# A two-layer adaLN trunk on one core: modulation weights read transposed and summed along the free axis, and the first products visited row block by row block

## The chip, the cores and the metric

One core of one Trainium2 chip runs the whole program. The metric is the device time of one execution in microseconds (us), as the median of the runs shown. Matrix products run on TensorE (PE in the rows, PEld its weight loads), elementwise work on VectorE (DVE) and ScalarE (ACT), a little on GpSimd (POOL). SyncE (SP) issues most loads.

## The reference, cut to what matters

```python
def reference(x, c, norm_w, mod_w, mod_b, a_w_in, a_w_out, b_w_in, b_w_out, final_norm_w):
    cond = jax.nn.silu(c)                              # c: (1, 2048)
    for i in range(2):                                 # x: (1, 256, 2048)
        mod = cond @ mod_w[i] + mod_b[i]               # mod_w[i]: (2048, 3 * 2048)
        shift, scale, gate = jnp.split(mod[:, None, :], 3, axis=-1)
        h = rms_norm(x, norm_w[i]) * (1.0 + scale) + shift
        # layer 0: ten projections of 2048 columns; layer 1: four
        y = (dilated_mixer(h, a_w_in[0], slopes) @ a_w_out[0] if i == 0
             else moba_mixer(h, b_w_in[0], slopes) @ b_w_out[0])
        x = x + gate * y
    return rms_norm(x, final_norm_w)
```

All data are float32. Each layer reads its weights once, and modulation weights of 2 x 2048 x 6144 numbers (100 MB of the 377 MB read) serve one product with a single vector each.

## The kernel before

**Data on the chip.** h is held transposed: hA has 16 row blocks of 128 (the model dimension, index k or kc) by 256 tokens, each as a high and a low part of float32r. A weight unit is two row blocks by 512 columns, 512 KB. `convert` loads it into `raw` (a pool of five buffers, `rawp`, that modulation blocks share), ScalarE copies it to `wh` (L376) and VectorE subtracts to get `wl` (L383, "split" below). Four pairs of wh and wl exist (`NB`). A product of a unit is three products on TensorE per tile (high by high, low by high, high by low).

**Steps.** The program is a list of steps, each some products of one unit, written out by hand in one loop at the end: the products, then tasks due at once (`at_once`: copying sums out), the splits, loads of new units by a plan, and tasks set for that step (`at`). The engines' queues keep this order. Layer A works in four column groups j of ten parts (v0 to v2, z, q0 to k2). The **first stage** takes the 16 first parts (`first_parts`: all of group 0, six of group 1) over only some row blocks at a time, since h's modulation is not known at the start: five strips of 2, 4, 4, 4 and 2 row blocks (`STRIPS`, in units 1, 2, 2, 2, 1). After each strip a part's sums go from PSUM to `act` (`evac_partial`: ScalarE copies for the first strip, VectorE adds, L591, for the other four). The rest of layer A, the output projection, layer B and its output follow.

**Modulation before.** `mod_w` lies with its 2048 inputs over partitions. For a block, VectorE multiplies each row of inputs by its value of silu(c) (`ccT`, one per partition) and adds to an accumulator `macc` (`mac`, L134 and L136). At the end the 128 partitions are added up: TensorE transposes, VectorE reduces (`column_sums`, L194 and L195). The very first strip is loaded by eight `start_unit`s of 256 columns, with some of the sums on TensorE (L157, L162); later strips by `strip_unit` while the strip before is worked on, and `strip_end` then makes hA's row blocks (L296 to L298). The gate of layer 0 and shift and scale of layer 1 come in six `piece_unit` sequences spread over the rest of layer A, from 16 steps after the first stage; the gate of layer 1 in two, in layer B's groups 1 and 2. The gate is summed over partitions and spread over them by products with ones (`gate_end`, `gate_add`).

**Attention.** Eight items per group (`item_a`), each in four tasks: scores (L472), softmax, transposes (L453), values (L490). The first group's items begin five steps before the end of the first stage.

Of the kernel before, what the change touches and what calls it, by code (L numbers as in the profile page):

```python
# [17 lines left out]
P = 128  # L18
S = 256
# [33 lines left out]
def trunk_kernel(ctx: ExitStack, tc: tile.TileContext, x, c, norm_w, mod_w, mod_b, a_w_in, a_w_out,  # L53
                 b_w_in, b_w_out, final_norm_w, dmask, out):
# [10 lines left out]
    maccp = pool("maccp", 2)  # L65
# [17 lines left out]
    rows = tp.tile([P, 512], F32, name="t")  # L83
    rows_c, rows_n, rows_b, cs = rows[:KC, 0:P], rows[:2 * KC, P:2 * P], rows[:96, 2 * P:3 * P], rows[:KC, 3 * P:]
    nc.scalar.dma_start(rows_c, c.rearrange("o (k p) -> (o k) p", p=P))
    nc.scalar.dma_start(rows_n, norm_w.rearrange("l (k p) -> (l k) p", p=P))
    nc.scalar.dma_start(rows_b, mod_b.rearrange("l (k p) -> (l k) p", p=P))
    gate = const.tile([P, D], F32, name="gate")
    dm = const.tile([P, 9 * P], F32, name="dm")
    ident = const.tile([P, P], F32, name="ident")  # L90
    make_identity(nc, ident)
    ones = const.tile([P, P], F32, name="ones")
    nc.gpsimd.memset(ones, 1.0)
# [4 lines left out]
    ccT = const.tile([P, KC], F32, name="ccT")  # L98
    nwT = const.tile([P, 2 * KC], F32, name="nwT")
    mbT = const.tile([P, 96], F32, name="mbT")  # L100
    abB = const.tile([P, 2 * KC], F32, name="abB")
    ssp = const.tile([P, 8], F32, name="ssp")

    nc.scalar.activation(cs, rows_c, AF.Silu)
    pst = ps_t.tile([P, 512], F32, name="pst", tag="t")
    nc.tensor.transpose(pst[:, 0:KC], cs, ident[:KC, :KC])
    nc.vector.tensor_copy(ccT, pst[:, 0:KC])

    def start_rows():
        psn = ps_y.tile([P, 512], F32, name="psy", tag="y")  # L110
        nc.tensor.transpose(psn[:, 16:48], rows_n, ident[:32, :32])
        nc.tensor.transpose(psn[:, 48:144], rows_b, ident[:96, :96])
        nc.vector.tensor_copy(nwT, psn[:, 16:48])
        nc.vector.tensor_copy(mbT, psn[:, 48:144])
        for l in range(2):
            m1 = mbT[:, 48 * l + 16:48 * l + 32]
            nc.vector.tensor_scalar(m1, m1, 1.0, None, op0=ALU.add)
# [14 lines left out]
    def mac(acc, raw, kc, first):  # L132
        if first:
            nc.vector.tensor_scalar(acc, raw, ccT[:, kc:kc + 1], None, op0=ALU.mult)  # L134
        else:
            nc.vector.scalar_tensor_tensor(acc, raw, ccT[:, kc:kc + 1], acc, op0=ALU.mult, op1=ALU.add)  # L136

    STRIPS = [1, 2, 2, 2, 1]
    strip_acc = {}

    start_ps = ps_t.tile([P, 512], F32, name="pst", tag="t")

    start_acc = maccp.tile([P, 1024], F32, name="macc", tag="macc")

    def start_unit(u):

        part, i = 1 - u // 4, u % 4
        raw = rawp.tile([P, 4, 256], F32, name="raw", tag="raw")
        src = mod_w[0, i * 512:(i + 1) * 512, part * D:part * D + 256]
        nc.sync.dma_start(raw, src.rearrange("(c p) n -> p c n", p=P))  # L150
        for k in range(4):
            kc = 4 * i + k
            if u < 4 or 4 <= kc < 14:
                mac(start_acc[:, part * 256:(part + 1) * 256], raw[:, k], kc, (u, k) in ((0, 0), (5, 0)))
                continue
            for b in range(2):
                nc.tensor.matmul(start_ps[:, b:b + 1], raw[:, k, b * P:(b + 1) * P], ccT[:, kc:kc + 1],  # L157
                                 start=u == 4 and k == 0 and b == 0, stop=False, skip_group_check=True)
# [710 lines left out]
```

## Time and profile before

| | |
|---|---|
| median of 3 runs | 1601.39 us (1598.77 to 1601.77) |
| the profiled execution | 1597.84 us, its span 1596.0 us |
| TensorE busy | 1561.0 us, 98% of the span |
| VectorE busy | 1173.8 us, 74% |
| ScalarE busy | 756.8 us, 47% |
| moved by DMA | 380.75 MB, 239 GB/s over the span |
| issues | 192 blocks of mod_w, 512 units of the four weights, 512 KB each |

The span goes from the first to the last instruction; the execution's own time is 1.8 us more. A TensorE instruction's duration includes a pipelined end that lies under the next one, so its pace is read from the starts of neighbours or from counts per window, not from durations.

### The profile page before, as it was taken

Reading aid. Unit: us, or ns where it says so; the run is one execution under the profiler, and the core shown is the slowest. Engines: PE = TensorE matmul, PEld = TensorE weight load, DVE = VectorE, ACT = ScalarE, POOL = GpSimd, SP = SyncE. Lnnn points to the kernel's source line nnn. Section 1 sums busy time; section 2 is a strip of 40 time slices with the busy share of each in tenths; the row PEclk is TensorE's granted clock in tenths of the full one; section 3 lists DMA queues with packets and bytes.
Section 4 is the critical chain, followed back from the end, with each engine's and each line's share of the span. In section 5 each row is a group of like instructions: output and inputs, shape, how many; then the busy total and the mean of one; then the engine's idle time right before and its main releaser. Section 6 shows DMA issues by size and latency. Waiting matters only on the chain.

```text
span 1596.0 us, 23586 instructions
## 1 busy us (share of the span) xinstructions
PE 1561.0 (98%) x9055; PEld 1376.4 (86%) x9055; DVE 1173.8 (74%) x1597; ACT 756.8 (47%) x1039; POOL 12.0 (1%) x29
## 2 busy tenths in 40 slices
PE   5999999999999999999999999999999999999997
PEld 4899999999888888888888888887888888888886
DVE  6899898878767776777776776766557877765665
ACT  4643334334544544444544444554445555455543
POOL 0000000000000000000000000000000000000000
PEclk9999999999999999999999999999999999999999
DMA  9988798866378768888778888456466877855553
GB/s 309 320 273 293 248 313 272 254 214 186 114 230 296 221 206 285 289 307 296 223 234 266 310 292 282 132 195 200 159 194 228 281 249 248 279 181 186 185 168 122
DMA packets 182240, 380.75 MB, mean 239 GB/s; under 512 B 11616, under 2 KB 19952, under 8 KB 181616
## 3 DMA queue, kind: packets, MB, share of 16 engines
q1 hardware_dynamic: 180352, 373.93, 71.6%
q0 software_dynamic: 1008, 4.19, 0.8%
q8 instruction: 71, 1.16, 0.3%
q10 hardware_dynamic: 768, 1.12, 0.2%
q14 instruction: 41, 0.34, 0.1%
HBM read 377.10 MB, written 2.10 MB: 238 GB/s over the span
## 4 chain that ended last, share of the span: by engine, by line
PE 92%; DMA 3%; DVE 3%; ACT 1%; issue 1%; POOL 0%; POOLq 0%; DVEq 0%; ACTq 0%
PE acc L335 27%; PE acc L338 14%; PE acc L313 10%; PE acc L311 10%; PE acc L312 10%; PE acc L326 4%; PE acc L325 4%; PE acc L324 4%; DMA raw<-in_mod_w_dram 2%; PE pss L472 2%; PE po L490 1%; PE pst L453 1%; DVE macc L136 1%; PE po L523 1%; PE pss L507 1%
## 5 line engine op out<-in xcount | busy, mean ns | idle before, releaser
L376 ACT ACTIVATE wh<-raw 128x1024 fp32r<-128x1024 f32 x504 | 528.1, 1058 | 536.7 <-PE acc L335 125.8
L383 DVE TENSOR_TENSOR wl<-raw,wh 128x1024 fp32r<-128x1024 f32 (+1 forms) x505 | 607.1, 1218 | 115.8 <-ACT wh L376 114.8
L335 PE MATMUL acc<-hA,wh 128*128 128x512 f32 x1152 | 302.9, 395 | 0.0
L136 DVE SCALAR_TENSOR_TENSOR macc<-raw,ccT,macc 128x1024 f32<-128x1024 f32 (+2 forms) x264 | 247.2, 936 | 48.5 <-DMA raw<-in_mod_w_dram 44.8
L335 PEld LDWEIGHTS acc<-hA,wh 128*128 128x128 f32 x1152 | 202.3, 189 | 32.0
L335 PE MATMUL acc<-hB,wh 128*128 128x512 f32 x768 | 203.4, 396 | 0.0
L324 PE MATMUL acc<-hA,wh 128*128 128x256 f32 x640 | 182.2, 285 | 0.6 <-ACT ext L589 0.4
L338 PEld LDWEIGHTS acc<-hA,wl 128*128 128x128 f32 x1152 | 166.8, 189 | 18.0
L326 PE MATMUL acc<-hA,wl 128*128 128x256 f32 x640 | 181.1, 283 | 0.0
L325 PE MATMUL acc<-hA,wh 128*128 128x256 f32 x640 | 181.1, 283 | 0.0
L338 PE MATMUL acc<-hA,wl 128*128 128x256 f32 x1152 | 171.8, 281 | 0.0
L311 PE MATMUL acc<-wh,hA 128*128 128x512 f32 x384 | 155.5, 405 | 4.2 <-ACT hA L296 1.5
L335 PEld LDWEIGHTS acc<-hB,wh 128*128 128x128 f32 x768 | 135.5, 189 | 21.8
L312 PE MATMUL acc<-wl,hA 128*128 128x512 f32 x384 | 151.1, 393 | 0.3 <-DVE wl L383 0.3
L313 PE MATMUL acc<-wh,hA 128*128 128x512 f32 x384 | 150.9, 393 | 0.0
L324 PEld LDWEIGHTS acc<-hA,wh 128*128 128x128 f32 x640 | 122.8, 192 | 1.6 <-ACT ext L589 0.7
L325 PEld LDWEIGHTS acc<-hA,wh 128*128 128x128 f32 x640 | 122.8, 192 | 0.4
L326 PEld LDWEIGHTS acc<-hA,wl 128*128 128x128 f32 x640 | 122.7, 192 | 0.0
L338 PEld LDWEIGHTS acc<-hB,wl 128*128 128x128 f32 x768 | 111.1, 189 | 12.1
L338 PE MATMUL acc<-hB,wl 128*128 128x256 f32 x768 | 114.5, 281 | 0.0
L311 PEld LDWEIGHTS acc<-wh,hA 128*128 128x128 f32 x384 | 73.0, 190 | 19.0 <-ACT actA1v L589 1.6
L313 PEld LDWEIGHTS acc<-wh,hA 128*128 128x128 f32 x384 | 72.8, 189 | 15.8
(235 smaller groups left out, 1680.8 us busy)
## 6 DMA issues: line engine op xcount, KB each, us to landing
raw<-in_a_w_in_dram SPq DMA_DIRECT2D x320, 512.0 KB, 4.8
raw<-in_mod_w_dram SPq DMA_DIRECT2D x192, 512.0 KB, 4.9
raw<-in_b_w_in_dram SPq DMA_DIRECT2D x128, 512.0 KB, 4.3
raw<-in_a_w_out_dram SPq DMA_DIRECT2D x32, 512.0 KB, 4.6
raw<-in_b_w_out_dram SPq DMA_DIRECT2D x32, 512.0 KB, 4.3
xin<-in_x_dram SPq DMA_DIRECT2D x2, 1024.0 KB, 9.2
x<-in_x_dram POOLq DMA_DIRECT2D x4, 512.0 KB, 5.8
gate<-in_mod_b_dram SPq DMA_DIRECT2D x1, 1024.0 KB, 7.8
```

The costliest lines, as they stand in the source:

```text
L136: nc.vector.scalar_tensor_tensor(acc, raw, ccT[:, kc:kc + 1], acc, op0=ALU.mult, op1=ALU.add)
L311: nc.tensor.matmul(o, hi, wh[:, i], start=f, stop=False, skip_group_check=True)
L312: nc.tensor.matmul(o, hi, wl[:, i], start=False, stop=False, skip_group_check=True)
L313: nc.tensor.matmul(o, lo, wh[:, i], start=False, stop=l, skip_group_check=True)
L324: nc.tensor.matmul(o, wh[:, i, wc], hi, start=f, stop=False, skip_group_check=True)
L325: nc.tensor.matmul(o, wh[:, i, wc], lo, start=False, stop=False, skip_group_check=True)
L326: nc.tensor.matmul(o, wl[:, i, wc], hi, start=False, stop=l, skip_group_check=True)
L335: nc.tensor.matmul(ps_of(h), ws[u][0][:, i, cols(h)], both, start=us[u] == 0 and i == 0, stop=False, skip_group_check=True)
L338: nc.tensor.matmul(ps_of(h)[:, 0:S], ws[u][1][:, i, cols(h)], st(2 * us[u] + i)[:, 0, :], start=False, stop=us[u] == 7 and i == 1, skip_gr ...
L376: nc.scalar.activation(wh, raw, AF.Copy)
L383: nc.vector.tensor_tensor(wl[:, c], raw[:, c], wh[:, c].bitcast(F32), op=ALU.subtract)
L472: nc.tensor.matmul(ps[:, n:n + w], heads_of("A", j, f"q{g}")[:, hh, tok], heads_of("A", j, f"k{g}")[:, hh, ks], start=True, stop=True)
```

## The change

1. **Modulation along the free axis.** The host transposes mod_w: `mod_t` has, per layer and block of 128 outputs, the outputs over partitions and the 2048 inputs along a row, in two halves of 4 KB per partition. `cb` holds silu(c) on all partitions, made by four products of a row of ones with c and four Silu. `mod_unit` loads a half and issues two `tensor_tensor_reduce` (multiply by cb, sum over 512), each of which becomes an ISA instruction of 128x512 and a second one of 128x1 that writes the sum into `modq`; a bias enters as the first sum's start. `mod_sums` adds four quarters. No transposes of sums, no `macc`. The gate's column is turned into rows by products of ones with diagonal matrices (`gate_split`, `gate_rows`).
2. **Visits.** The first 16 parts are worked half-unit by half-unit (one row block by 512 columns). The table `READY` says at which half-step row block k is ready (0, 9, 18, 28, 39, 50, 62, then every 12 up to 170). A visit takes the part that is furthest behind as far as rows are ready. This gives 55 visits of 1 to 10 row blocks, where the strips had 80; 16 are first ones (copied by ScalarE), 39 add (23 of them by half-step 170). Row block k has its four modulation blocks between READY[k - 1] and READY[k], then `rows_ready(k)`: a sum, a product with the norm's weight, two ScalarE operations for hA's high part and the full value, one subtraction.
3. **Order and layout.** `weights` holds all units in the order of use, a unit as 4 KB per partition; before, a unit was two pieces of 2 KB per partition. x is loaded first, then four modulation blocks, then weights. Six scalings of x move from VectorE to POOL. The attention items of the first group begin at half-step 217 of 256, and the later pieces at half-step 170, spread to 12 steps before layer A's output. The gate of layer 1 comes in 64 steps on end.

The number of products of h with weights is the same, and so is the number of bytes of weights.

```diff
-    def strip_unit(s, u):
...
-        nc.sync.dma_start(raw, mod_w[0, i * n * P:(i + 1) * n * P, n0:n0 + w].rearrange("(c p) n -> p c n", p=P))
-        for k in range(n):
-            mac(strip_acc[s][:, part * w:(part + 1) * w], raw[:, k], i * n + k, i == 0 and k == 0)
+    for i, (p, t) in enumerate(zip((ps_y, ps_t, ps_s, ps_o), "ytso")):
+        pcb = p.tile([P, 512], F32, name="pcb", tag=t)
+        nc.tensor.matmul(pcb, ones[0:1], c_row[i // 2][0:1, i % 2 * 512:(i % 2 + 1) * 512], start=True, stop=True)
+        nc.scalar.activation(cb[:, i * 512:(i + 1) * 512], pcb, AF.Silu)
+    def mod_unit(layer, b, half):
+        raw = rawp.tile([P, 1024], F32, name="raw", tag="raw")
+        nc.sync.dma_start(raw, mod_t[layer, b, half])
+        m = 48 * layer + b
+        for i in range(2):
+            part, q = raw[:, i * 512:(i + 1) * 512], 2 * half + i
+            nc.vector.tensor_tensor_reduce(part, part, cb[:, q * 512:(q + 1) * 512], 1.0, 0.0 if q else mbT[:, m:m + 1],
+                                           ALU.mult, ALU.add, modq[:, m, q:q + 1])
+    def mod_sums(m, n, step=1):
+        cols = slice(m, m + (n - 1) * step + 1, step)
+        nc.vector.tensor_reduce(modc[:, cols], modq[:, cols], axis=AX.X, op=ALU.add)
...
         if g:
-            nc.vector.tensor_scalar(xc, xc, start_r[tt][:, 0:1], None, op0=ALU.mult)
+            nc.gpsimd.tensor_scalar(xc, xc, start_r[tt][:, 0:1], None, op0=ALU.mult)
...
+    def rows_ready(k):
+        mod_sums(k, 2, 16)
+        sc, sh = sc0[:, k:k + 1], modc[:, k:k + 1]
+        nc.vector.tensor_tensor(sc, modc[:, 16 + k:17 + k], nwT[:, k:k + 1], op=ALU.mult)
+        src = xnT[k // 8][:, k % 8]
+        hf = tmpp.tile([P, S], F32, name="hf", tag="tmp")
+        nc.scalar.activation(hA[:, k, 0], src, AF.Identity, scale=sc, bias=sh)
+        nc.scalar.activation(hf, src, AF.Identity, scale=sc, bias=sh)
+        nc.vector.tensor_tensor(hA[:, k, 1], hf, hA[:, k, 0].bitcast(F32), op=ALU.subtract)
...
-        nc.sync.dma_start(raw, units[n]["src"])
+        nc.sync.dma_start(raw, weights[n].rearrange("p (c n) -> p c n", c=2))
...
+    for n in (9, 9, 10, 11, 11) + (12,) * 10:
+        READY.append(READY[-1] + n)
...
+        n = done.index(min(done)) if n_ready < KC else next(i for i, d in enumerate(done) if d < KC)
+        k0 = done[n]
+        while done[n] < KC and READY[done[n]] <= t:
+            done[n] += 1
+            t += 1
+        visits.append((n, k0, done[n]))
...
+    for k in range(1, KC):
+        i0, i1 = READY[k - 1], READY[k]
+        for n in range(4):
+            at(i0 + n * (i1 - i0 - 3) // 4, mod_unit, 0, (16 if n < 2 else 0) + k, n % 2)
+        at(i1 - 3, rows_ready, k)
...
-            base = i0 - 5 + i if j == 1 else i0 + 1 + 2 * i
+            base = first_group_end + 2 + 3 * i if j == 1 else i0 + 1 + 2 * i
...
-    span = (first_end + 16, len(steps) - 8)
+    span = (READY[-1], len(steps) - 12)
```

Three places in the engines' queues, in program order. The first is SP's queue at its start, where the names are destination and source; before:

```order
L150 DMA raw<-in_mod_w_dram 128x4x256 x2
L253 DMA xin_107<-in_x_dram 128x2048
L150 DMA raw<-in_mod_w_dram 128x4x256
L253 DMA xin_108<-in_x_dram 128x2048
L150 DMA raw<-in_mod_w_dram 128x4x256 x5
L370 DMA raw<-in_a_w_in_dram 128x2x512 x5
```

and of the change:

```order
L192 DMA xin_104<-in_x_dram 128x2048
L192 DMA xin_105<-in_x_dram 128x2048
L130 DMA raw<-in_mod_t_dram 128x1024 x4
L298 DMA raw<-in_weights_dram 128x1024 x4
L130 DMA raw<-in_mod_t_dram 128x1024
```

x now stands first, and four blocks, not eight, stand ahead of the weights, so the first unit takes the fifth buffer.

The second is ScalarE's queue from its table load to the second set of weights (cb is the spread silu(c), pcb its product, sq the squares of x, pxt the transposes of x); before:

```order
L104 ACT_TABLE_LOAD
L104 ACTIVATE t<-t 16x128
L257 ACTIVATE sq,ss_151<-xin_107 128x1024 x2
L267 ACTIVATE xin_107<-xin_107,rstd 128x512
L257 ACTIVATE sq,ss_168<-xin_108 128x1024 x2
L267 ACTIVATE xin_108<-xin_108,rstd 128x512
L274 ACTIVATE xnT_105<-pxt 128x4x128 x2
L376 ACTIVATE wh<-raw 128x1024
L296 ACTIVATE hA<-xnT_105,ab 128x256 x2
```

and of the change:

```order
L109 ACT_TABLE_LOAD
L109 ACTIVATE cb<-pcb 128x512 x4
L196 ACTIVATE sq,ss_147<-xin_104 128x1024 x2
L196 ACTIVATE sq,ss_157<-xin_105 128x1024 x2
L206 ACTIVATE xin_104<-xin_104,rstd 128x512
L213 ACTIVATE xnT_102<-pxt 128x4x128
L206 ACTIVATE xin_105<-xin_105,rstd 128x512
L213 ACTIVATE xnT_102<-pxt 128x4x128
L305 ACTIVATE wh<-raw 128x512 x2
L225 ACTIVATE hA<-xnT_102,modc,sc_128 128x256
```

Four operations of 512 columns stand ahead of the squares in place of one of 128, and each copy of transposes now stands between the two scalings.

The third is VectorE's queue inside the first stage, in its first third (numbers tell the buffers apart; acc is PSUM, actA0v0 and actA1v1 are partial sums of parts); before, at the start of the second strip:

```order
L383 TENSOR_TENSOR wl_893<-raw_890,wh_892 128x1024
L134 TENSOR_SCALAR macc_915<-raw_916,ccT_126 128x512
L136 SCALAR_TENSOR_TENSOR macc_915<-raw_916,ccT_126,macc_915 128x512
L591 TENSOR_TENSOR actA0v0_287<-actA0v0_287,acc_895 128x512
L591 TENSOR_TENSOR actA0v0_287<-actA0v0_287,acc_896 128x512
L383 TENSOR_TENSOR wl_913<-raw_910,wh_912 128x1024
L136 SCALAR_TENSOR_TENSOR macc_915<-raw_940,ccT_126,macc_915 128x512 x2
```

and of the change, around one `rows_ready`:

```order
L523 TENSOR_TENSOR actA1v1_557<-actA1v1_557,acc_1557 128x512
L523 TENSOR_TENSOR actA1v1_557<-actA1v1_557,acc_1558 128x512
L312 TENSOR_TENSOR wl_1612<-raw_1609,wh_1611 128x1024
L140 TENSOR_REDUCE modc_127<-modq_126 128x2
L222 TENSOR_TENSOR sc0_128<-modc_127,smalls_110 128x1
L227 TENSOR_TENSOR hA_145<-hf_1638,hA_145 128x256
L312 TENSOR_TENSOR wl_1634<-raw_1631,wh_1633 128x1024
L312 TENSOR_TENSOR wl_1658<-raw_1655,wh_1657 128x1024
L134 ISA raw_1667,modq_126<-raw_1667,cb_125,smalls_110 128x512
L134 ISA modq_126 128x1
L134 ISA raw_1667,modq_126<-raw_1667,cb_125 128x512
```

A block's two operations became two pairs, and the row blocks become ready one at a time between the splits, where before four came together at a strip's end.

## Rows read from the trace of the kernel before

**Rows 1.** The page: engines' busy time; VectorE's tenths in 40 slices.

```profile
PE 1561.0 (98%) x9055; PEld 1376.4 (86%) x9055; DVE 1173.8 (74%) x1597; ACT 756.8 (47%) x1039; POOL 12.0 (1%) x29
...
DVE  6899898878767776777776776766557877765665
```

**Rows 2.** Windows: length, busy by engine (instructions), granted clock, DMA share, GB/s.

```profile
0.00:10.00 10.00, 0.25 (x1) 0.18 (x1) 4.15 (x10) 2.03 (x3) 0.87 (x8) 1.00 0.83 286
10.00:20.00 10.00, 5.26 (x23) 4.66 (x24) 6.42 (x17) 5.98 (x11) 2.54 (x6) 1.00 1.03 349
...
25.70:84.30 58.60, 53.56 (x344) 47.78 (x344) 49.51 (x69) 37.11 (x56) 0.00 (x0) 0.97 0.93 314
84.30:410.30 326.00, 325.02 (x2255) 304.73 (x2255) 289.75 (x394) 135.55 (x142) 0.00 (x0) 1.00 0.78 252
```

**Rows 3.** Timeline of the start: start, us, engine, line, [idle before, releaser].

```profile
4.00 0.31 ACT L104 ACTIVATE t<-t 16x128 f32<-16x128 f32 x1 [0.42 <-DMA t<-in_c_dram]
...
9.56 1.06 ACT L257 ACTIVATE sq<-xin 128x1024 f32<-128x1024 f32 x1 [5.26 <-DMA xin<-in_x_dram]
10.53 0.19 ACT L257 ACTIVATION_READ_ACCUMULATOR sq<-xin 128x1 f32 x1
...
20.02 3.67 SPq L370 DMA_DIRECT2D raw<-in_a_w_in_dram  x5
...
24.09 1.06 ACT L376 ACTIVATE wh<-raw 128x1024 fp32r<-128x1024 f32 x1 [2.51 <-DMA raw<-in_a_w_in_dram]
...
25.69 0.80 PE L311 MATMUL acc<-wh,hA 128*128 128x512 f32 x1 [1.54 <-ACT hA L296]
...
28.07 3.49 DVE L383 TENSOR_TENSOR wl<-raw,wh 128x1024 fp32r<-128x1024 f32 x3
```

**Rows 4.** TensorE's pace: one window of 256-column products, then its timeline.

```profile
210.00:220.00 10.00, 10.00 (x86) 1.00 0.92 303
...
35.66 0.77 PE L273 MATMUL pxt<-ident,xin 128*128 128x128 f32 x4 [2.24 <-DVE xin L265]
...
330.19 0.39 PE L311 MATMUL acc<-wh,hA 128*128 128x512 f32 x1
330.42 0.39 PE L312 MATMUL acc<-wl,hA 128*128 128x512 f32 x1
...
409.01 0.66 PE L453 MATMUL pst<-ident,t 128*128 128x128 f32 x4 [0.30 <-ACT pT L455]
409.50 1.04 PE L472 MATMUL pss<-actA0k,actA0q 128*128 128x256 f32 x6
410.30 1.17 PE L335 MATMUL acc<-hA,wh 128*128 128x512 f32 x4
```

**Rows 5.** Groups by form, 0 to 420 us: count, busy us, mean ns, idle.

```profile
L383 DVE TENSOR_TENSOR wl<-raw,wh 128x1024 fp32r<-128x1024 f32 x131 | 157.4, 1218 | 1.6 <-ACT wh L376 1.5
...
L136 DVE SCALAR_TENSOR_TENSOR macc<-raw,ccT,macc 128x512 f32<-128x512 f32 x90 | 67.5, 750 | 11.9 <-DMA raw<-in_mod_w_dram 10.0
...
L591 DVE TENSOR_TENSOR ext<-ext,acc 128x512 f32<-128x512 f32 x32 | 21.1, 682 | 9.8 <-PE acc L326 9.4 <-PE acc L313 0.4
...
L437 DVE TENSOR_REDUCE m<-t 128x1 f32<-128x512 f32 x6 | 4.1, 685 | 0.2
L435 DVE SCALAR_TENSOR_TENSOR t<-dm,pss 128x512 f32<-128x512 f32 x6 | 4.1, 680 | 0.0
...
L448 DVE TENSOR_SCALAR t<-t,rl 128x512 f32<-128x512 f32 x5 | 2.4, 487 | 0.2
```

**Rows 6.** The same view, 430 to 1150 us.

```profile
L136 DVE SCALAR_TENSOR_TENSOR macc<-raw,ccT,macc 128x1024 f32<-128x1024 f32 x90 | 115.2, 1280 | 27.6 <-DMA raw<-in_mod_w_dram 27.5
```

**Rows 7.** Windows of VectorE alone: busy, granted clock, DMA share, GB/s.

```profile
200.00:220.00 20.00, 19.39 (x24) 1.00 0.93 311
...
1230.00:1240.00 10.00, 8.94 (x16) 1.00 0.75 244
```

**Rows 8.** DMA queues, 430 to 830 us: packets, MB, share of 16 engines.

```profile
q1 hardware_dynamic: 44641, 102.12, 78.1%
```

More of the change, by code (lines that the diff above doesn't have):

```diff
@@ L145, in start_unit @@
[L145 to L158, printed above, removed]
@@ L197, in gate_end @@
-    def gate_end(layer, half, n):
-        acc = piece_acc[layer, 2, half][:, n * 512:(n + 1) * 512]
-        hi, lo = (tp.tile([P, 512], F32R, name="t") for _ in range(2))
-        nc.scalar.activation(hi, acc, AF.Copy)
-        nc.vector.tensor_tensor(lo, acc, hi.bitcast(F32), op=ALU.subtract)
-        gate_parts[n] = (hi, lo)
-    def gate_add(half, n):
-        pg = ps_y.tile([P, 512], F32, name="psy", tag="y")
-        for i in range(2):
-            nc.tensor.matmul(pg, ones_r, gate_parts[n][i], start=i == 0, stop=i == 1)
-        g = gate[:, half * 1024 + n * 512:half * 1024 + (n + 1) * 512]
-        nc.vector.tensor_tensor(g, g, pg, op=ALU.add)
@@ new lines, in gate_rows @@
+    def gate_rows(layer, n):
+        pg = ps_y.tile([P, 512], F32, name="psy", tag="y")
+        for i, part in enumerate(gate_cols[layer]):
+            diag = tp.tile([P, 4, P], F32R, name="t")
+            for b in range(4):
+                nc.vector.tensor_scalar(diag[:, b], ident, part[:, 4 * n + b:4 * n + b + 1], None, op0=ALU.mult)
+            nc.tensor.matmul(pg, ones_r, diag.rearrange("p b q -> p (b q)"), start=i == 0, stop=i == 1)
+        nc.scalar.activation(gate[:, n * 512:(n + 1) * 512], pg, AF.Copy)
@@ L375, in convert @@
             wh, wl = (slot(i, "held", F32R).rearrange("p (c n) -> p c n", c=2) for i in units[n]["hold"])
-        nc.scalar.activation(wh, raw, AF.Copy)
+        for c in [slice(0, 1), slice(1, 2)] if halves else [slice(0, 2)]:
+            nc.scalar.activation(wh[:, c], raw[:, c], AF.Copy)
         to_finish.append((raw, wh, wl))
@@ L618, in trunk_kernel @@
-    first_end = len(steps)
+    READY = [0]
+    for n in (9, 9, 10, 11, 11) + (12,) * 10:
+        READY.append(READY[-1] + n)
+    done = [0] * len(first_parts)
+    visits, t = [], 0
+    while min(done) < KC:
+        n_ready = sum(r <= t for r in READY)
+        n = done.index(min(done)) if n_ready < KC else next(i for i, d in enumerate(done) if d < KC)
[4 more added lines that the diff above has]
+        visits.append((n, k0, done[n]))
```

285 lines of the change are left out of this document (108 added, 177 removed).

## The prediction

> **What bounds the kernel now.** I read the page first: TensorE is busy 98% of the span and VectorE 74%, but VectorE's slices show that it is at eight or nine tenths in the first quarter and at five to seven later [rows 1]. So after the start every microsecond is TensorE's, and the first quarter is where another engine could take over. The windows split that quarter [rows 2]. Up to 25.7 us there are no products. From 25.7 to 84.3 (the first strip, 16 parts over two row blocks) TensorE is busy 53.6 of 58.6 us and the DMA engines 93% of the time, at 314 GB/s. From 84.3 to 410.3 TensorE never pauses for long and VectorE is busy 290 of 326 us. Then the timeline of the start [rows 3]: the first weight block is issued only at 20.02 us, because eight blocks of modulation weights stand ahead of it in five buffers; it lands at 24.09, and the first product starts at 25.69. The granted clock averages 0.97 over those 58.6 us [rows 2]: TensorE, idle before, spent about 3.5 us at the lower of its two clocks (1.2 GHz).
>
> How much of the stage from 25.69 to 410.30 is work? 1920 products of 256 columns, of which 86 fit in 10 us [rows 4], are 223 us; 576 of 512 columns at a spacing of 0.227 us [rows 4] are 131; together 354. The 24 transposes of x are at most 0.17 us each (4 in 0.77 with the last one's end) [rows 4], 4.1 us; the 28 transposes of sums some 0.12 (four of attention take 0.49 until the next starts), 3.4 us. An attention item has scores (0.80 us until the next starts), four transposes (0.49) and values with as many column passes as the scores (taken as 0.95) [rows 4]: 2.25 us, 18 for the first eight. By 410.30 five scores, three sets of transposes and one of values are done, 6.4 us. That makes 368 of 384.6 us. **So 16.7 us of the stage are lost, most of it in the first strip,** which holds 32 half-steps of 354/256 = 1.383 us, the 24 transposes and a few sums (49.5 us) in 58.6.
>
> **The start.** Removed: four of the eight first modulation blocks ahead of the weights, 24 one-column products and 8 sums of one column on TensorE, the transposes of bias rows. Added: four products that spread c over all partitions, four Silu, x first in SP's queue. Two arms lead to the first product. By transfers: x (2.1 MB) and four blocks of 0.524 MB at the rates of the first two windows (286, then 349 GB/s) [rows 2] are there at 13.8 us; two new VectorE pairs (below) and two small operations end at about 16. By ScalarE: c is there at 4.00, as the first Silu shows [rows 3]; a product of 512 plain float columns has the column passes of one item's scores, 0.8 to 0.9 us [rows 4], and double at the lower clock: two at either clock make 5.2. ScalarE takes 1.06 us for 1024 columns [rows 3], so some 0.6 for 512: the last Silu ends near 10. Then ScalarE's queue in its new order: four squares of 1.06 and a read of 0.19 each, overlapping a little [rows 3] (4.8), a scaling (0.6), four transposes at the lower clock (1.2), a copy (0.6), the same three again, two halves of the weights (1.2) and hA's first row block (0.4): 21.2 us, and the first product at about **21.5**, 4.2 us sooner. ScalarE, not the weights, is late next. The six scalings moved to POOL have no row there; ready to start near 16, they may take 1.2 us each, over twice what 512 columns cost ScalarE, before TensorE's step 2 (24.3 us) needs the first two, and the last is not needed before step 12. Cost: nothing, a microsecond if POOL is slower still.
>
> **The unknown price.** The change's core is VectorE's new operation: multiply two 512-wide tensors and sum them, followed by a second one that writes the sum, 128x1. No row of before shows either. Bounds: at the bottom the two-tensor operation of 512 at 0.682 (a partial sum's addition) and a hidden second part, 0.68 us together [rows 5]; at the top the two-tensor operation with a scalar, 0.750 [rows 5], with a second part like ScalarE's, 0.19 [rows 3], 0.94 together. I take 0.72 + 0.08 = **0.80**: the shape is that of the operation with a scalar, and neighbours on VectorE overlap by some 0.05 us (three splits of 1.218 in 3.49 us) [rows 3, 5]. A block of 512 KB then costs 1.60 us, against 1.50 for two operations in a strip and 1.28 in the later pieces [rows 5, 6].
>
> **The first stage, three engines against each other.** It falls into 170 half-steps in which rows still come in, and 86 after.
>
> TensorE: 170 x 1.383 + 4.1 = 239 us. VectorE: 85 splits at 1.163 (99 us), 60 blocks at 1.60 (96), 15 row blocks with a subtraction of 256 columns (0.41 by the line through 512 and 1024) and two small operations, some 0.7 together (11), and 23 visits that add to an earlier partial, two additions of 0.682 each [rows 5] (31): 237 us. DMA: 148 blocks and the masks, 78.2 MB; the windows give 314 at 93% and 252 at 78% [rows 2], so 323 to 338 GB/s when full, 231 to 242 us. All three within 4%.
>
> The last 86: TensorE 119 + 18 for the eight attention items, which now all fall in here, 137 us; VectorE 50 for splits, 39 for the 24 blocks of later pieces that now start here, 22 for 16 visits, and 22 for the items (0.685 + 0.680 + 0.487 and some 0.9 for four short ones) [rows 5]: 133 us.
>
> Sums: TensorE 376, VectorE 370, where before had 49.5 + 289.8 = 339 in 385 us [rows 2]. What VectorE loses is the sums over strips: 64 x 2 additions become 39 x 2. What it gains back is the 24 blocks and the items. The highest load that it held before with no harm to TensorE is 19.39 of 20 us [rows 7], 97%; 370/0.97 = 381 us. I add 4.5 us, half of the first strip's loss, since in the first 29 half-steps (44 us for TensorE) ScalarE has 42 us of work, VectorE 39 and the DMA 43. **Stage: 386 us, end at 407.5.** Before reaches the same work (410.3 and 11.6 us of items) at 421.9. Gain 14.4.
>
> **Later.** Gone are 32 more transposes of sums for layer B, in a place with no idle time, 0.12 each as above: 3.8 us. The gate's 16 products remain. In layer B 32 blocks come in 64 steps on end, each 0.32 us dearer; VectorE is at 8.9 of 10 us there at most [rows 7], and one more microsecond in ten just fits. I charge 2 us. In layer A's rest the blocks are sparser than before (72 over some 500 us, by the steps, against 96 in 480), no charge.
>
> The larger rows of a transfer (4 KB in place of 1 and 2) I price at nothing: with short rows alone the rate per busy share was 323 to 338 GB/s [rows 2], and from 430 to 830 us, where a third of the blocks had long ones, 102.1 MB at 78.1% are 327 [rows 8]. If they help, the DMA line above falls by some per cent, and it does not set the sum.
>
> **Sum.** 14.4 + 3.8 - 2 = 16.2 us off the profiled execution's 1597.8; the median of three runs is 3.6 us above it, 1601.4, and from that I get **1585 us** (-1.0%).
>
> **Rivals.**
> - *VectorE becomes the bound (slower).* Place: the whole first stage, 168 new pairs. Each 0.1 us more is 17 us. The gain is gone at 0.90 us; at 0.94 VectorE has 394 us, the stage takes 410 and the kernel about 1609. For it: VectorE's load is within 2% of TensorE's, and the second instruction has no row. Against: the first is like an operation measured at 0.75.
> - *The sum halves the rate.* From rows: 512 more columns cost the operation with a scalar 0.53 us [rows 5, 6], 1.04 ns each; an operation that also sums might need twice that, 1.25 us and 0.04 for its hidden second part. VectorE then has 452 us in the first stage, which ends 71 us later than before, and is over in layer B by some 25: about 1694. The Trainium skill (Vector Engine (DVE) Microarchitecture Reference, "Points that are easy to get wrong") says that the scalar form with two SBUF sources wider than bf16 halves its throughput, since no port is left for the accumulator. By that rule this would be the case; the trace shows no halving for that form without a sum, and no run yet shows it with one.
> - *Transfers set the pace.* Five raw buffers now hold what three engines at 97% release. If the stage runs at the first strip's 314 GB/s, its 78.2 MB take 249 us, ten more than TensorE; with a similar slip at the visits' ends the gain shrinks to 0 to 9 us: 1592 to 1601. For it: the first strip did just this. Against: from 84 us on the DMA had slack.
> - *No loss at all.* TensorE's 376 us from 21.5, nothing charged for layer B: 1573.
>
> **How the numbers follow.** Forecast (10 to 25 us gained) 0.50; no loss 0.06; transfers 0.20, of which half is within 0.2% of before, about what a measurement of this kernel can tell from no change; VectorE the bound 0.18, a sixth of it within 0.2%; halved 0.06. Faster 0.66, same 0.13, slower 0.21. For the range I leave out the halved rate and the outer tails: from no loss, 1573, to the top price, 1609.
>
> **What would show it.** First product near 21.5 us, after ScalarE's hA. New pairs of 0.75 to 0.85 us. TensorE's first stage of 380 to 392 us, its idle time within the first 60 us; VectorE at 95% or more there. No transposes of sums. The prediction is wrong if a pair costs 0.9 or more, if TensorE waits for hA or for weights all through the 170 half-steps, or if layer B's 64 steps show TensorE idle.

## The result, and the profile after

The changed kernel takes 1619.3 us (median of 4 runs, 1615.8 to 1621.2) beside 1600.1 us for the kernel before on the same chip (1598.2 to 1601.8): the ratio is 1.0118, 95% interval 1.0095 to 1.0141. It is slower by 1.2%, where 1.0% faster was forecast. The profiled execution took 1618.21 us.

The page of the changed kernel, against [rows 1]:

```profile
PE 1567.0 (97%) x8968; PEld 1371.5 (85%) x8968; DVE 1130.0 (70%) x2052; ACT 767.3 (47%) x1061; POOL 23.2 (1%) x34
...
PE   6999999999998999999999999999999999899997
...
DVE  5788888978775766766766765765448887465665
...
PEclk9999999999998999999999999999999999999999
```

VectorE has less to do than before, TensorE 87 instructions fewer. What is new are two dents in TensorE's slices, at about 490 and 1390 us, of which the first shows in the granted clock too. In both, VectorE is idler than around them: it holds TensorE up with little work. The waits of TensorE name it (us in total, times, longest):

```profile
PE psy L159 <- DVE t L158: 17.1, 11, 3.3
...
PE po L419 <- ACT pT L384: 2.4, 4, 0.9
```

`psy L159` is the gate's product, which waits for the diagonals that `gate_rows` has VectorE make in the line above it. Before, the gate's 16 products (L207) waited for nothing. The view of their line names no idle time of TensorE ahead of them (nothing stands between the two headings):

```profile
L207 PE MATMUL psy<-t,ones_r x16: 393/396/477, 563.6 to 1392.7; 128*128 128x512 f32 x16
its engine sat idle before it (us, times) until:
who waited for it (us, times):
```

TensorE's timeline at the stages' ends (first product; last products of the first stage and first ones of the first whole part, that is, of a part that is worked over all 16 row blocks at once; first product of layer A's output, of layer B, of layer B's output):

```profile
21.04 0.80 PE L238 MATMUL acc<-wh,hA 128*128 128x512 f32 x1 [2.21 <-ACT hA L225]
...
418.93 0.28 PE L249 MATMUL acc<-hA,wh 128*128 128x256 f32 x1
419.05 0.28 PE L250 MATMUL acc<-hA,wh 128*128 128x256 f32 x1
419.17 0.28 PE L251 MATMUL acc<-hA,wl 128*128 128x256 f32 x1
419.29 0.63 PE L260 MATMUL acc<-hA,wh 128*128 128x512 f32 x2
...
1005.97 0.40 PE L238 MATMUL acc<-wh,yA 128*128 128x512 f32 x1
...
1113.19 0.40 PE L238 MATMUL acc<-held,hB 128*128 128x512 f32 x1
...
1512.73 0.40 PE L238 MATMUL acc<-wh,yB 128*128 128x512 f32 x1
```

The start came as forecast (21.04; forecast 21.5). The first stage ends at 419.29, not at 407.5; before, the same work was done at 421.9. So 2.6 of the 14.4 us are there. Before, layer A's output, layer B and its output begin here:

```profile
999.36 0.40 PE L311 MATMUL acc<-wh,yA 128*128 128x512 f32 x1
...
1106.26 0.39 PE L311 MATMUL acc<-held,hB 128*128 128x512 f32 x1
...
1492.81 0.40 PE L311 MATMUL acc<-wh,yB 128*128 128x512 f32 x1
```

The rest of layer A, 589.1 us before, should have shrunk by the items that moved out of it (11.6) and the transposes of sums (3.8) to 573.7, and takes 586.7. Layer B should have stayed at 386.6, and takes 399.5. Both lost 13.0 us, each where its gate is made. The three engines' timelines at the second set of gate rows (a set is eight diagonals and the two products with them; each layer has four):

```profile
482.59 0.63 PE L263 MATMUL acc<-hA,wl 128*128 128x256 f32 x4
...
483.26 0.38 ACT L505 ACTIVATE actA1q<-acc 128x256 f32<-128x256 f32 x1 [1.23 <-PE acc L263]
...
483.68 0.42 DVE L506 TENSOR_TENSOR actA1q<-actA1q,acc 128x256 f32<-128x256 f32 x1 [3.98 <-ACT actA1q L505]
484.02 1.22 DVE L312 TENSOR_TENSOR wl<-raw,wh 128x1024 fp32r<-128x1024 f32 x1
485.15 1.65 DVE L158 TENSOR_SCALAR t<-ident,gate 128x128 fp32r<-128x128 f32 x8
...
486.16 0.47 PE L159 MATMUL psy<-t,ones_r 128*128 128x512 f32 x1 [2.94 <-DVE t L158]
```

This is the whole mechanism. A whole part's four heads (128 columns each) end one after the other in its last four steps, and one of them ends in this step. Its addition (L506) stands at the head of VectorE's queue and waits for ScalarE's copy (L505), which waits for this step's products. VectorE idles 3.98 us; then come the addition, a weight split and the diagonals, one after the other. TensorE has the gate's product next in its own queue, which is in order as well, and stands for 2.94 us with all later products behind it. Of the eight sets of gate rows, five stand so behind a head's addition and wait 1.80 to 3.31 us; one in layer B waits 2.96 us behind two weight splits that were late themselves; two (at 478.08 and 1375.33 us), where VectorE began the diagonals over a microsecond before TensorE came to the products, do not wait.

The idle time is not all. The windows of the two stretches, of the changed kernel (length, busy by engine, granted clock, DMA share, GB/s):

```profile
476.00:512.00 36.00, 27.27 (x120) 22.09 (x119) 18.71 (x52) 10.98 (x15) 0.00 (x0) 0.86 0.42 140
1365.00:1400.00 35.00, 26.49 (x124) 21.52 (x123) 17.34 (x44) 11.74 (x17) 0.00 (x0) 0.90 0.38 127
```

A mean clock of 0.86 over 36 us means that 10 us went at 1.2 GHz in place of 2.4; 0.90 over 35 us, 7 us. At half speed that loses 5.0 and 3.5 us on top of 17.1 us of waits: 25.6 us.

The other new thing, the first stage, by groups (0 to 420 us, as [rows 5]) and by windows:

```profile
L312 DVE TENSOR_TENSOR wl<-raw,wh 128x1024 fp32r<-128x1024 f32 x130 | 158.6, 1227 | 29.2 <-ACT wh L305 28.6
...
L134 DVE CUSTOM_DVE_ANT_0 raw<-raw,cb 128x512 f32<-128x512 f32 x133 | 87.7, 685 | 2.8 <-DMA raw<-in_mod_t_dram 2.7
...
L134 DVE CUSTOM_DVE_ANT_0 raw<-raw,cb,smalls 128x512 f32<-128x512 f32 x45 | 33.5, 745 | 3.9 <-DMA raw<-in_mod_t_dram 2.9 <-ACT cb L109 1.0
L134 DVE DVE_READ_ACCUMULATOR2_ANT modq<- 128x1 f32 x177 | 14.4, 81 | 0.0
...
L204 POOL TENSOR_SCALAR xin<-xin,rstd 128x512 f32<-128x512 f32 x6 | 11.0, 1842 | 0.0
...
L227 DVE TENSOR_TENSOR hA<-hf,hA 128x256 fp32r<-128x256 f32 x16 | 6.8, 425 | 24.4 <-ACT hf L226 24.4
```

```profile
21.00:80.00 59.00, 55.79 (x350) 49.58 (x351) 46.46 (x92) 43.54 (x65) 6.18 (x3) 1.00 0.83 289
80.00:112.00 32.00, 29.66 (x217) 28.59 (x216) 28.12 (x56) 12.33 (x15) 0.00 (x0) 0.95 0.84 281
112.00:345.00 233.00, 232.14 (x1631) 218.18 (x1630) 200.99 (x374) 97.68 (x104) 0.00 (x0) 1.00 0.88 307
345.00:419.00 74.00, 71.44 (x470) 63.96 (x469) 61.08 (x126) 35.34 (x54) 0.00 (x0) 1.00 0.62 209
```

The multiply-and-sum costs 0.685 us, 0.745 with the bias, and its read of 0.081 lies mostly under the next one (sums in a row start 0.61 us apart, 398.74 and 399.35 by the reads). VectorE is busy 337 of 398 us (third busy column), but it also stands 24.4 us for ScalarE's `hf`, of which 5.4 lie ahead of the first product, and 28.6 for ScalarE's `wh`: 385 us inside the stage, in an engine that works in order. TensorE idles 9.0 us, nearly all before 112 and after 345 us, and from 80 to 112 us 0.95 is the clock.

### The profile page after: what moved, and what is told of

The parts are those of the page before. It is cut to its first block, busy times and chain, and to the rows that moved or that the text cites. A ratio compares the mean times of both kernels' runs of the same rounds, so it can differ in the third digit from the quotient of the medians.

```text
span 1616.4 us, 23816 instructions
## 1 busy us (share of the span) xinstructions
PE 1567.0 (97%) x8968; PEld 1371.5 (85%) x8968; DVE 1130.0 (70%) x2052; ACT 767.3 (47%) x1061; POOL 23.2 (1%) x34
## 5 line engine op out<-in xcount | busy, mean ns | idle before, releaser
L305 ACT ACTIVATE wh<-raw 128x1024 fp32r<-128x1024 f32 (+1 forms) x505 | 526.6, 1055 | 520.6 <-PE acc L260 182.1
L312 DVE TENSOR_TENSOR wl<-raw,wh 128x1024 fp32r<-128x1024 f32 (+1 forms) x505 | 609.3, 1221 | 185.4 <-ACT wh L305 183.7
L134 DVE CUSTOM_DVE_ANT_0 raw<-raw,cb 128x512 f32<-128x512 f32 x288 | 190.0, 685 | 7.8 <-DMA raw<-in_mod_t_dram 7.8
L263 PEld LDWEIGHTS acc<-hB,wl 128*128 128x128 f32 x768 | 112.1, 191 | 12.3
```

Of the source, the lines that this page charges most:

```text
L134: nc.vector.tensor_tensor_reduce(part, part, cb[:, q * 512:(q + 1) * 512], 1.0, 0.0 if q else mbT[:, m:m + 1], ALU.mult, ALU.add, modq[:, ...
L263: nc.tensor.matmul(ps_of(h)[:, 0:S], ws[u][1][:, i, cols(h)], st(2 * us[u] + i)[:, 0, :], start=False, stop=us[u] == 7 and i == 1, skip_gr ...
L305: nc.scalar.activation(wh[:, c], raw[:, c], AF.Copy)
L312: nc.vector.tensor_tensor(wl[:, c], raw[:, c], wh[:, c].bitcast(F32), op=ALU.subtract)
```

## The experiments

Theory G: the gate's diagonals and product in one task cost the 25 us. Rival P: layer B's new VectorE work does it, by itself. For the first stage: D, transfers; V, VectorE's load and its waits in order.

The stage column of this table goes from the first product to the first whole-part product, from each profile's timeline; the interval is of the ratio to the kernel before.

| kernel | us | ratio, 95% | first stage, us |
|---|---|---|---|
| changed | 1619.3 | 1.0095 to 1.0141 | 21.04 to 419.29: 398.3 |
| e1_gate_two_tasks | 1590.65 | 0.9936 to 0.9966 | 21.03 to 417.69: 396.7 |
| e2_rows_two_tasks | 1617.27 | 1.0103 to 1.0133 | 21.02 to 414.47: 393.5 |
| e4_before_laid_out | 1599.03 | 0.9991 to 1.001 | 25.52 to 409.60 (before: 25.69 to 410.30) |
| e5_gate_and_rows | 1589.15 | 0.9928 to 0.9961 | 21.30 to 416.34: 395.0 |
| e6_gate_clear_steps | 1596.43 | 0.9979 to 0.9998 | 21.04 to 416.84: 395.8 |
| e7_half_the_bytes | 1588.0 | 0.9919 to 0.9948 | 21.03 to 415.02: 394.0 |
| e8_short_reductions | 1581.42 | 0.9882 to 0.9911 | 22.10 to 411.27: 389.2 |
| e9_rows_every_12 | 1600.22 | 1.0000 to 1.0019 | 21.02 to 424.36: 403.3 |
| e10_values_later | 1590.2 | 0.9931 to 0.9958 | 21.07 to 417.72: 396.7 |
| e12_sums_by_stt | 1590.17 | 0.9932 to 0.9963 | 21.15 to 417.98: 396.8 |
| e13_rows_on_pool | 1592.8 | 0.9950 to 0.9977 | 21.08 to 419.26: 398.2 |
| e14_gate_rows_values | 1587.24 | 0.9915 to 0.9940 | 21.00 to 413.68: 392.7 |

Up to the end of the first stage, the changed kernel, e1 and e6 have the same instructions, and their profiles give 395.8 to 398.3 us for it. So a difference of up to some 2.5 us between two stages, of one profile each, shows nothing.

**The gate in two tasks.** All eight diagonals of a set are made in one step, the products follow two steps later:

```diff
+    def gate_diag(layer, n):
...
-                at(i1 + 4 + 2 * n, gate_rows, layer, n)
+                at(i1 + 4 + 2 * n, gate_diag, layer, n)
+                at(i1 + 6 + 2 * n, gate_rows, layer, n)
```

> The changed kernel, with gate_rows split in two tasks: VectorE's diagonal matrices at the old step, TensorE's products with them two steps later. Theory G (the gate's products stand in TensorE's queue directly behind VectorE work that itself stands behind a head's addition, and each such wait also costs 3.4 us at the lower clock): the 17.1 us of waits of the gate's products go to under 2 us, five of the six late stretches at clock 0.5 vanish, and the time falls by 24 to 28 us, to about 1593 us, 0.4% under before. Rival P (the pieces of modulation weights, dearer or denser than before, slow the later stages, and the gate's waits are only where that shows): the waits move to other products, and the time stays within 6 us of 1619.

It took 28.7 us off the changed kernel, 0.7 more than G's band. Its wait for the diagonals, and its windows over the same steps:

```profile
PE psy L164 <- DVE t L158: 0.4, 2, 0.2
```

```profile
476.00:512.00 36.00, 35.47 (x196) 30.14 (x195) 25.69 (x64) 16.04 (x23) 0.00 (x0) 1.00 0.70 237
1337.00:1372.00 35.00, 34.86 (x200) 30.30 (x199) 25.56 (x63) 18.66 (x28) 0.00 (x0) 1.00 0.59 199
```

TensorE is busy throughout at full clock. Its timeline shows the stages' ends:

```profile
417.69 0.40 PE L266 MATMUL acc<-hA,wh 128*128 128x512 f32 x1
...
990.93 0.40 PE L244 MATMUL acc<-wh,yA 128*128 128x512 f32 x1
...
1098.15 0.40 PE L244 MATMUL acc<-held,hB 128*128 128x512 f32 x1
...
1485.00 0.40 PE L244 MATMUL acc<-wh,yB 128*128 128x512 f32 x1
```

From the first whole part to layer A's output it takes 573.2 us (changed: 586.7), and for layer B 386.85 (changed: 399.5, before: 386.55). Layer B's new pairs are all still there, so rival P falls: they cost nothing that can be seen.

**One task, other steps.** This asks whether one task is the trouble by itself, or what stands ahead of it on VectorE:

```diff
-                at(i1 + 4 + 2 * n, gate_rows, layer, n)
+                at(i1 + (4, 5, 6, 7)[n] if layer else i1 + (4, 5, 14, 15)[n], gate_rows, layer, n)
```

> The changed kernel with diagonals and products of the gate left in one task, but at steps in which no head ends (eight steps moved in all; nothing else changes). Theory H (TensorE waits because VectorE's diagonals stand behind a head's addition that itself waits for this step's products): no wait over 1 us for the diagonals is left, TensorE's clock stays up, and the kernel takes 1588 to 1595 us, as with two tasks. Rival T (one task is the trouble by itself, since TensorE comes to its product as soon as VectorE begins the diagonals): each of the eight waits remains at about the 1.65 us that a set of diagonals takes, and the kernel takes 1605 to 1620.

22.9 us off, 1.4 us above the band for H and far from T's. Six of the eight sets have moved. Seven wait 0.9 us or less; one long wait is left, in layer B. VectorE's and TensorE's timelines around it:

```profile
1351.87 2.36 DVE L312 TENSOR_TENSOR wl<-raw,wh 128x1024 fp32r<-128x1024 f32 x2 [0.78 <-ACT wh L305]
1354.15 1.65 DVE L158 TENSOR_SCALAR t<-ident,gate 128x128 fp32r<-128x128 f32 x8
...
1355.08 1.58 PE L159 MATMUL psy<-t,ones_r 128*128 128x512 f32 x2 [2.96 <-DVE t L158]
1356.45 2.88 PE L260 MATMUL acc<-hB,wh 128*128 128x512 f32 x8
```

No head's addition stands there, but two weight splits do, which had waited for ScalarE. So T falls, and H holds in a wider form: one task is safe where VectorE's queue is ahead of TensorE, and costs the whole lag where it is not, whatever made the lag. The eight products behind the wait take 2.88 us, where eight take 2.02 at the upper clock (at 1362.70 us in the changed kernel). Layer B takes 392.6 us, 5.7 more than in e1, and the whole kernel 5.8 more.

**Row blocks in two tasks.** The subtraction that waits for `hf` moves one step later, here with the gate as in the changed kernel:

```diff
+    def rows_low(k):
...
         at(i1 - 3, rows_ready, k)
+        at(i1 - 2, rows_low, k)
```

> The changed kernel, with rows_ready split: the subtraction that VectorE does for hA's low part one step later, so that a split stands between it and ScalarE's work on which it waits. Theory V (VectorE's 24 us of waiting for hf in its own queue delays splits and frees raw buffers late, and costs the first stage some 5 to 10 us): VectorE's wait for hf falls under 8 us and the first stage (first product to the first product of a whole part, 398 us) gets 4 us or more shorter. Rival T (transfers set the pace of the rows): the wait goes, the first stage stays within 2 us, VectorE idles for transfers instead.

The wait for `hf` falls from 24.4 to 7.3 us (6.2 of them for the first row block), that of the splits for `wh` rises from 183.7 to 193.4 (over the span). The stage is 4.8 us shorter than the changed kernel's, as V said, but only 2.3 shorter than that of e6, which has the changed kernel's first stage. The total moves by 2 us, within the two intervals. With the gate mended as well:

> Both splits in one kernel. Theories G and V: 1593 less 4 to 8 us, 1585 to 1589 us. G alone: the same as with the gate split alone, within 2 us. P: near 1615.

1.5 us below the gate alone, and the stage is 1.6 shorter: both are within the noise. So it helps little or not, and that VectorE's wait for `hf` costs the stage 4 us is not shown.

**Layout alone.** The kernel before, with its weights laid out by use in 4 KB rows and nothing else:

```diff
-        src = w[u * 256:(u + 1) * 256, n0:n0 + GC].rearrange("(c p) n -> p c n", p=P)
+        src = weights[len(units)].rearrange("p (c n) -> p c n", c=2)
...
```

> The kernel before, with one part of the change alone: the weights laid out in the order of use, 4 KB per partition and unit in place of two pieces of 2 KB. If longer rows raise the rate (first strip above 330 GB/s in place of 314, and weights landing in under 4.5 us): the first strip is 3 us or more shorter, 1596 us or less. If not, as the prediction priced it: within 2 us of before.

No change, with an interval of 0.1% to either side. The share of busy DMA engines in the first strip's window falls from 0.93 to 0.89 at the same 314 GB/s.

**What the first stage lacks.** Half of each modulation block's bytes, or three quarters of each sum's columns, left out, both with the gate in two tasks:

```diff
-        nc.sync.dma_start(raw, mod_t[layer, b, half])
+        nc.sync.dma_start(raw[:, :512], mod_t[layer, b, half][:, :512])
...
-            part, q = raw[:, i * 512:(i + 1) * 512], 2 * half + i
-            nc.vector.tensor_tensor_reduce(part, part, cb[:, q * 512:(q + 1) * 512], 1.0, 0.0 if q else mbT[:, m:m + 1],
+            part, q = raw[:, :512], 2 * half + i
+            nc.vector.tensor_tensor_reduce(raw[:, 512:], part, cb[:, q * 512:(q + 1) * 512], 1.0, 0.0 if q else mbT[:, m:m + 1],
...
```

> On top of the gate in two tasks: of each block of modulation weights only the first half is loaded, and both sums are made from it, so the output is not the reference's; all instructions of VectorE, ScalarE and TensorE stay. In the first stage 22 of 78 MB of transfers go. Theory D (what the first stage takes beyond the forecast 386 us is late transfers): the stage from first product to first whole-part product falls from 397 to 388 us or less, the kernel to 1578 to 1583. Rival V (VectorE's queue, or waits between ScalarE and VectorE): within 2 us of the kernel with two tasks, 1589 to 1592.

```diff
-            nc.vector.tensor_tensor_reduce(part, part, cb[:, q * 512:(q + 1) * 512], 1.0,
+            part = part[:, :128]
+            nc.vector.tensor_tensor_reduce(part, part, cb[:, q * 512:q * 512 + 128], 1.0,
```

> On top of the gate in two tasks: the multiply-and-sum takes 128 of its 512 columns, so the output is not the reference's; transfers and the count of instructions stay. Some 0.4 us of 0.61 go per sum, 0.8 us per block, 65 us of VectorE's time in the first stage. Theory V (VectorE's load makes TensorE late there): the first stage falls from 397 to 388 us or less, the kernel to 1575 to 1583. Theory D (transfers): within 2 us, 1589 to 1592. If both this and half the bytes gain some 5 us each, the two share the loss: what is late is the block as a whole, landing and reduction one after the other.

With half the bytes the stage is 2.7 us shorter, and the time lies between the two bands. With short sums the stage is 7.5 us shorter, and the time is in V's band, though the stage is 1.2 us above V's 388. So VectorE's load makes the stage longer; whether TensorE then lacks the split itself or a block that came late because its buffer came free late, this does not tell. D's share stays open: 2.7 us is hardly more than the spread, and the edit gives VectorE more to do. Both sums now write the same half of `raw`, the second starts some 0.11 us later, and VectorE is busy 343 us of the stage in place of 337. The windows and the splits' group (20 to 420 us) of the kernel with short sums:

```profile
21.00:80.00 59.00, 56.54 (x355) 50.56 (x356) 37.12 (x96) 44.58 (x68) 7.24 (x4) 1.00 0.83 294
80.00:112.00 32.00, 30.74 (x243) 29.88 (x243) 23.70 (x59) 13.21 (x15) 0.00 (x0) 1.00 0.90 303
112.00:345.00 233.00, 233.00 (x1626) 219.00 (x1625) 163.69 (x378) 100.07 (x107) 0.00 (x0) 1.00 0.85 308
345.00:419.00 74.00, 73.70 (x488) 66.54 (x487) 53.87 (x128) 34.84 (x53) 0.00 (x0) 1.00 0.66 223
```

```profile
L319 DVE TENSOR_TENSOR wl<-raw,wh 128x1024 fp32r<-128x1024 f32 x133 | 162.6, 1229 | 68.9 <-ACT wh L312 68.3
```

VectorE's busy time is 58 us below the changed kernel's, and 40 of them turn into waits for `wh`. This kernel's first product came only at 22.10 us, so 1.1 us of the first window lie ahead of the stage. TensorE gains where it lost: before 112 us, and from 345 on, where the attention items stand.

**Row blocks due later.**

```diff
-    for n in (9, 9, 10, 11, 11) + (12,) * 10:
+    for n in (12,) * 15:
```

> On top of the gate in two tasks: row blocks are due every 12 half-steps from the start (180 in all) in place of 9, 9, 10, 11, 11 and then 12 (170). With 9 half-steps TensorE has 12.4 us of work while 8.5 blocks of 0.524 MB come in, 13.5 us at 330 GB/s; with 12 it has 16.6 us for 10 blocks, 15.9 us. Theory E (the early row blocks are due faster than transfers bring them): of the some 12 us lost between 21 and 112 us 5 to 8 go, the kernel takes 1582 to 1587, and more visits (additions of 0.68 us on VectorE) cost nothing. Rival: the losses come from waits inside a row block's preparation, whatever its due time; within 2 us of the kernel with two tasks.

Wrong by 13 us and more: the kernel takes 9.6 us more than with the gate alone, its first stage 6.7. Its window where the stage of the others ends:

```profile
345.00:419.00 74.00, 68.98 (x467) 63.16 (x466) 63.27 (x127) 33.43 (x49) 0.00 (x0) 0.98 0.68 221
```

The plan now makes 70 visits in place of 55, each further one two additions of 0.68 us on VectorE, some 20 us. Up to 112 us TensorE is busy as long as with the gate alone (85.9 of 91 us), and from 112 to 419 it idles 7.5 us in place of 2.5. Theory E falls. More VectorE work goes with a longer stage, which points to V again, though the due times moved as well. Even two tasks do not always save the gate: VectorE, still late, keeps a product of the gate waiting to 500.04 us, for 1.35, though its task is two steps later than that of the diagonals, and the ten us from 500 on have a mean clock of 0.83.

**Attention items.**

```diff
-            item_a(j - 1, i // 2, i % 2, base, (0, 2, 4, 6) if j == 1 else (0, 1, 3, 5))
+            item_a(j - 1, i // 2, i % 2, base, (0, 2, 4, 7) if j == 1 else (0, 1, 3, 5))
```

> On top of the gate in two tasks: the values of the first eight attention items come one half-step (1.4 us) later after their transposes. Their waits for ScalarE's copy of the transposed scores are 3.4 us in the first stage of the changed kernel. Theory A (these waits are lost time, since in this stage the steps are half as long as where the items stood before): 2 to 4 us off, 1586 to 1589. Rival: the queue of VectorE is behind anyway and TensorE waits elsewhere; no change, 1589.5 to 1592.

The wait for `pT` (2.4 us in the changed kernel, not the 3.4 that I expected) is down to 0.2, and a new one stands an operation earlier in the item, for VectorE's normalization:

```profile
PE pst L388 <- DVE t L383: 2.0, 2, 1.5
```

No change in time: the rival.

**The sum by the scalar form.** Three of four sums:

```diff
+            if q:
+                nc.vector.scalar_tensor_tensor(part, part, 1.0, cb[:, q * 512:(q + 1) * 512], op0=ALU.mult, op1=ALU.mult,
+                                               accum_out=modq[:, m, q:q + 1])
...
```

> On top of the gate in two tasks: three of four sums are made by the two-tensor operation with a scalar (here the constant 1) that also accumulates, in place of the custom multiply-and-sum; the fourth keeps the custom one for its bias. This is the form of which the prediction's rival said that a sum might halve its rate. Halved: each such sum takes about 1.25 us in place of 0.61; VectorE gets some 80 us more in the first stage, which it does not have, and the kernel takes 1650 or more. Not halved: 0.75 and a hidden read, 0.65 to 0.70 from start to start; 5 to 11 us more on VectorE in the first stage, and 1591 to 1597.

Not halved, and 0.8 us under the band for that. Its group, over the whole span:

```profile
L135 DVE SCALAR_TENSOR_TENSOR raw<-raw,cb 128x512 f32<-128x512 f32 x288 | 190.2, 686 | 10.0 <-DMA raw<-in_mod_t_dram 9.8
```

**The subtraction on POOL.**

```diff
-        nc.vector.tensor_tensor(hA[:, k, 1], hf, hA[:, k, 0].bitcast(F32), op=ALU.subtract)
+        nc.gpsimd.tensor_tensor(hA[:, k, 1], hf, hA[:, k, 0].bitcast(F32), op=ALU.subtract)
```

> On top of the gate in two tasks: the subtraction that makes a row block's low part goes to POOL, which is idle then. VectorE's queue loses 15 operations of about 0.4 us and 15 waits of about 1.2 us for ScalarE's hf, 24 us in all. Theory Q (time in which VectorE stands or works in order is what the first stage lacks; 65 us less work gave 7.5 us): the stage shrinks by 2 to 4 us, the kernel takes 1586 to 1589. Rival: POOL, which took 1.83 us for 512 columns, is so late with the low part (about 0.9 us against 0.4) that TensorE waits for it; no gain, 1590 to 1595.

The rival's side, 1592.8, but not for its reason alone. POOL's group and two waits of TensorE:

```profile
L233 POOL TENSOR_TENSOR hA<-hf,hA 128x256 fp32r<-128x256 f32 x16 | 12.1, 753 | 238.0 <-ACT hf L232 238.0
```

```profile
PE pxt L218 <- POOL xin L210: 2.7, 1, 2.7
...
PE acc L256 <- POOL hA L233: 0.9, 1, 0.9
```

The second row block's subtraction stands in POOL's queue between the first three scalings of x and the last three. It waits 10.8 us for ScalarE's `hf`, to 38.97 us, and so a transposition of x at 41.30 waits 2.7 us for its scaling. From 38 to 50 us TensorE is busy 9.3 us at a mean clock of 0.86, where with the gate alone it is busy 11.6 at 1.00. Theory Q is not decided by this run: what VectorE gave back may have been spent there.

**Together.** Gate, row blocks and values:

> All that helped so far together: gate in two tasks, the row blocks' subtraction one step later, and the first items' values one half-step later. If the gains add: 1.5 us below the gate alone for the rows and 2 to 4 for the values, 1584 to 1588; if VectorE's queue takes back what the values give, 1588 to 1590.

1587.24 us, 0.9915 to 0.9940 of the kernel before: the lowest median of the kernels that leave nothing out, though its interval touches that of the gate alone (0.9936 to 0.9966). Its stage is 392.7 us, 4.0 less than with the gate alone. Its clock from 80 to 112 us is 1.00 (with the gate alone 0.95), but so it is in e6, with the changed kernel's own first stage.

## Why the prediction was wrong, point by point

**The step that failed: "The gate's 16 products remain", costed at nothing.** The products did remain, but what they wait for was new. Before, `gate_end` and `gate_add` were two steps apart; the change puts VectorE's eight diagonals and TensorE's product into one task, and does it in steps in which heads end. I wrote of the products and not of the wait that was added, nor named what stood ahead of it on VectorE. By the medians e1 takes 28.7 us off, by the two ratios to the kernel before 26.7, by the profiled executions 27.7. Of these last, 1.6 lie in the first stage, where the edit changes nothing. The other 26.1, 13.4 in layer A and 12.7 in layer B, are the gate's; the trace of the changed kernel gave 25.6 (17.1 of waits, 8.5 of lower clock). By the forecast's own sum, 1585 + 26 is 1611, outside the range by that step alone. The profiled executions add up: 1618.2 us is 36.6 above the forecast for it (1597.8 less 16.2), of which the gate has 26.1 and the first stage 12.3 (398.3 for 386); all else is 1.8 us better than forecast.

**The first stage, 386 us, was mis-sized;** with the gate mended it takes 396.7. The step has three terms.

- *TensorE's work.* I took 86 products in 10 us from [rows 4] for the pace. That count includes products that reach in over both ends of the window. Starts are 0.12 us apart, as 418.93, 419.05 and 419.17 show, so 1920 products are 230 us, not 223, and the work 383. The loss of the kernel before was then 9.6 us, not 16.7: much of what I meant to recover was work.
- *VectorE's load.* 370 us was too much by the pair's price: 0.61 from start to start in place of 0.80, times 168, is 32 us, and 337 were measured. But I divided by 0.97, a limit from a stretch in which VectorE hardly waits, and counted no waits. Inside the stage it stands 48 us for ScalarE, and 337 + 48 is 385. So two errors nearly cancel, and it is luck that my 381 lies near that. I had not named the wait for `hf`.
- *The charge of 4.5 us.* TensorE's idle time and lower clock make 10.6 us in the changed kernel and 9.3 with the gate in two tasks (e1). Of the 13.7 between 383 and e1's 396.7, short sums take 7.5 away (e8), and half the bytes 2.7 (e7), which is not clear of noise; the two may overlap. In e8 6.2 us are left, of which 2.9 are idle time; the rest no run took apart.

**Right:** the start, 21.04 for 21.5, with ScalarE's arm last; POOL's scalings hidden, though they took 1.84 us each, beyond my bound of 1.2; the 32 transposes of sums, in the 573.2 us of layer A's rest in e1 (573.7 by the forecast); the long rows at nothing (e4). The 2 us for layer B were not needed: 386.85 us (e1) for 386.55. Two of the signs that I had named failed: VectorE is busy 85% of the stage, not 95, and 2.6 us of TensorE's idle time lie behind 345 us.

**The rivals.** The measured time lies outside the range, on the slow side, for a reason that was no rival. *VectorE the bound* has the place, not the price: a pair far below the break-even of 0.90, yet it is VectorE's load that lengthens the stage (e8). *The sum halves the rate*: it does so in neither form, 0.685 us for the custom one and 0.686 for the scalar form with a sum (e12); without a sum the scalar form takes 0.750 on two SBUF sources, and a two-tensor addition 0.682 [rows 5]. The Trainium skill (Vector Engine (DVE) Microarchitecture Reference, "Points that are easy to get wrong") says that the scalar form with two non-bf16 SBUF sources halves its throughput, with no port left for the accumulator. No run here shows that, and the measurement decides. *Transfers*: 2.7 us at most seen (e7), and their share is not settled. *No loss*: fell.

## What to carry to other kernels

When a change puts a producer on one engine and its consumer on another into one task, look at the producer's queue at that very step, not at its load: an engine that is busy half of the time (18.7 of 36 us here) can be 3 us late, if its queue's head waits for the consumer's own products. Give the consumer's task a later step: here that held the diagonals two steps longer and cost no time (e1), though it does not help where the producer is later still (e9). Count an engine's waits in order along with its work before calling it free, and take a pace from neighbours' starts, not from a count per window.

## What the runs showed of the hardware

- Behind waits of 1.8 to 3.3 us TensorE was often, not always, granted the lower clock for a while: about 17 us over two sets of four gate rows, 8.5 us lost. After the wait that ended at 1368.63 it was not: the window from there to 1375.20 us shows 1.00. In e9 it fell behind a wait of 1.35 us (0.83 over ten us).
- The custom multiply-and-sum over 512 float columns takes as long as a plain two-tensor operation (0.685 against 0.682 us [rows 5]), and its read of 81 ns lies under the next sum (sums start 0.61 us apart). The scalar form with a sum takes 0.686 (e12).
- POOL took 1.84 us to scale 512 columns by a column, and 0.753 us to subtract 256 (e13); ScalarE scales 512 in 0.71 in the same stretch, and VectorE took 0.481 for the same six scalings before.
